# adaLN's first products and column sums in four 32-row places, and attention's scores of a head pair in two 64-row places of TensorE's array

## The chip, the cores and the metric

The kernel runs on one core of one Trainium2 chip. A core has a matrix engine (TensorE, PE in the profile), three engines for element-wise work (VectorE, DVE; ScalarE, ACT; GpSimd, POOL) and queues that start DMA transfers (SP's above all). Each engine works through its own list of instructions in order and waits on semaphores for the others. The metric is the time of one execution on the device in microseconds, the median of several runs.

## What is computed

A trunk of two layers over 512 latent tokens (a grid of 8 rows by 64) and 256 context tokens, width 1024. In each layer a vector per stream (latent or context) is turned into shift, scale and gate of two sub-layers, which is what is called adaLN here:

```python
mod_lat = (silu_c @ ada_w[i] + ada_b[i])[:, None, :]      # ada_w[i]: 1024 x 6144
mod_ctx = (silu_cc @ ada_w[i] + ada_b[i])[None, None, :]
h_lat = modulate(rmsnorm(x, norm_g[i, 0]), sh1, sc1)      # x * (1 + scale) + shift
```

Layer 0 mixes tokens by attention beside a spatial gating unit, layer 1 by retention; each is followed by a gated feed-forward part with a convolution over three tokens. In attention each of eight heads of width 64 takes a softmax over a window of the grid (with a bias and a mask) together with all context keys; context tokens attend to each other:

```python
s_nb = einsum('brqhd,brkhd->bhrqk', qg, k_blk) * scale    # window, + bias, masked
s_cx = einsum('brqhd,bchd->bhrqc', qg, k_ctx) * scale     # context keys
p = softmax(concatenate([s_nb, s_cx]))                    # one softmax over both
```

All data is float32.

## The kernel before, in words

PE multiplies float32 in two ways here. A *native* f32 matmul takes the operands as they are. The other form takes operands rounded to a shorter type (fp32r): a value x is split into hi, its rounded part, and lo = x - hi, by `split` (line 170): ACT writes hi (L171), DVE writes lo (L172). `mm3` (L216 to L218) then sums hi·hi, hi·lo and lo·hi, three matmuls for one product. Tokens are in six tiles of 128 (0 to 3 latent, 4 and 5 context); the contraction dimension lies on the 128 rows of the array.

The stages, in the order of the span: the first products of adaLN with the input projection of the gating unit (`sgu`, to about 150 us), attention (to about 345 us), feed-forward of layer 0, retention, feed-forward of layer 1.

**First products** (`ada_first`, L246). Shift and scale of the first sub-layer are needed before any projection. They are made in four quarters q of the width, each with n = 0 (shift) and n = 1 (scale), each from two weight tiles of 128 x 1024 (kp = 0, 1) holding four blocks k of the contraction. The stationary operand is the conditioning vector's block for both streams, two columns wide (`cs`, L266), the moving one 256 columns of weights; eight matmuls k = 0..7 add up into rows 0 and 1 of a PSUM tile `ad`. Quarters 0 and 1 are native. Quarters 2 and 3 split the weights into `ah` and `al` (1024 wide, on ACT and DVE) and use four columns `c4` (hi and lo of both streams) at L268 and L269. Then ACT copies the rows to `mr` (L273), two small transposes turn them into columns (`adt`, L276), and DVE adds the bias (L284, L286) into `ab`. The products of quarter q + 1 are laid between the projection matmuls `ug` of quarter q in `sgu`; `first_h` scales and splits the tokens for quarter q.

**Later column sums** (`ada_half`, L311). The other shifts, scales and gates are made in the background, a half (512 columns) at a time: DVE multiplies weight tiles by the conditioning vector, one scalar for each row, and adds them up in `acc` (128 x 512, one for each stream, L326). What is left is a sum over the 128 rows. For shifts and scales (12 halves; 8 with two streams, 4 with one) `acc` is split, and matmuls with a two-column selector `sel` (L364) add hi and lo of each stream into row s of `ac`; ACT copies the rows (L366), four transposes (`at`, L370) make columns of them, DVE writes `ab` (L375, L377). Gates are summed with a matrix of ones (L347, L348). These jobs (`bg`) lie between the pieces of `sgu`, attention, both feed-forward parts and retention.

**Attention** (L909). Heads come in pairs j that share a projection: q, k, v of a pair are 128 rows, 64 for each head. `take_qk` (L997) splits them from PSUM, 64 rows at a time: for each head a tile q with hi in rows 0 to 63 and lo in rows 64 to 127, a tile `ka` with k's hi in both halves, and `kb` with k's lo in both, the second half copied by POOL (L1021). So one matmul with `ka` and one with `kb`, each over all 128 rows, give all four products of hi and lo (`score`, L1066, L1067). A block b of a head is 128 query positions: blocks 0 to 3 take 256 window keys and 256 context keys, block 4 the context's own scores, each two matmul pairs into one bank of PSUM (tag B, two banks). DVE adds bias and mask (L1103), finds the least (L1113), ACT takes the exponential (L1122). `weigh` (L1126) follows two blocks later: four transposes (L1136, L1160), a copy by ACT (L1137, L1162), and the product with v in native f32, 64 columns wide, blocks 0 and 1 into rows 0 to 63 of the PSUM tile `o` and blocks 2 and 3 into rows 64 to 127 (L1144 to L1151), once per head; `oc` (L1167) for block 4. The result is split into `at`, 64 rows at a time.

**rms** (L405) adds two partial sums of squares on POOL (L408); POOL then takes the power (L389).

**Order.** The program text gives an order of instructions; `queue` (near the end) replaces each engine's order, and that of the DMAs it starts, by the one in the packed table `ORDER`: for each of PE, DVE, ACT, POOL and SP a list of steps through its instructions.

Of the kernel before, what the change touches and what calls it, by code (L numbers as in the profile page):

```python
# [18 lines left out]
P = 128  # L19
# [37 lines left out]
oBE^h?c}z-ak`$vB|Q9&PqQv3mYD&$*Wq*>fawyZ``woEv$%$z$0HPo&TJgIy{;Zb3sPgTFSB(y41P{#JEHS5aELB=Z}vnav-s}pg0oO(mKLA80q
|Y!J6!ILpC|FO5O*R$9ecKaYBR5RCZvzDi$4G#W`eqf=vRf8Q33#al-=|V4l#%!%0tN|XP9#&R&@D=;l=Jns9HoYdkWwtJb8QLm6O@vc9AJ(*d!0
+_I^7usKHWk>G0od_dhszlPwu%59|Nf@9-s(S@aX>O0oSu+kS%^Bb58|CcO?{WW9cceQ5~MQDdHr-hVU^-=zpPN1gVavHjuLPJ9`=3mf9uxAf_ZS
YSDsAHa4Tt|9@)&~!HO%IdM$Vg7-G&kp>}Pe%DZ2mi_?qg5m4u_~z-e33KZZ#npD4!)OmVVAx1RJ8cv`LH|7O!u|-JRcn#Mb)Fn;vwcL^RZ(?iS0  # L60
+T(zOV7!W@zhd)M|jxR350iLo`)2k0;xS%Pu6nrUvV1j8LYHIJ&SL^3^*&;)(#5ZR-+!d=+f&I8m--%L$vXTmJ*hT||XrVZMkaPW7@P|v_;2X^|k
{?A|Ih6gwoeLpZ^_?g6#(uVBet}k<MaJv)wA5B;Z{Cq-VATmBtijaCSodQk>H*8wB(kq`FiWLVMj8LtypHF9DV$h12aIijz#Wlu~97wc0A78N%Ay
cC5Z2Wz4oYr2Cr20lywx8qP|1YuZ{yr<h!^4+e0cOZ{Y+6zRc+j_=6a9JTA?x^dN~3bqDGp*Cz<0Rsa&&O+tGHV#{^?*g-{w|NXRghvt(*BB1t-Y
%Je8fvUvQB}=Q>=^=;q!1qfd|3MgGQFgN~P2h`ZXE6P3t$661kM?!1zjecY-!C-W0%v#zvawJ>t?{Cnb98`G!t!8q~vdAv|vg55M`WR^jm%_=|n@
xc+92E!h{njJqY_ow>%Spl7nY_s3$>6P0P986E$a&gE@6PS&^;t5Pe8*5lrXoE*CcSn?WJ*Gc-hLy={4&+F-h1xm?_hs$>J$ZZ4IvGJ^CA6De$v|
2|G^id6a4K`?*dVT~rBV0!0W-cZLM+9Rdv8QtkHSNK#@af=CQLxsSsm+;ebAlBT4Mo@9^R}(1b@JxUrx4bactPhs`>DhN%5u{OFp8tTiX{Oixa|W
M%#LD{6u`uhd<9H`5qqJVo1M`hO1a_>F!xJ`Ga}kB|usl{LY%v-gfMpAA(n53NQW)-sxAlMBeE@sYIIb3@-J<2peo+ae(8y{iK0~zMT;i8ujU&fu
_d7*CVmwx2wsxD<i2`qdpGxo*jp(N0O{8vhnxcJt0pT3A9Bf-}9sCNNly8388;{qr-{aI$k8u?CdYxo2EH#YNfStxZ6n~)J$Q$bs8du0^3`5R-}<
Oi>2YD^44P`K_MRh=Gk1z@xW**bSq0TGHN-4aP%qe!Hj%beI~TCIF!1pG&Q6Rrkm9vF>XYxsmokGVhs;;V?%#GytF|_;Oz3=1c^U4;2gI}R8LLlv
!CQQvCV~q3%ijnk0mBq>4(35W<Q;?)VFBj1S{Q*>Hc);mSal<Lny~i)3{6(nH0VGxVhhXkjbaM&;4a=3wxLG>yNpZYyW^_>C=<XuoExl`agZ=RfG  # L70
d$6!nKWZu?0x_Hd?saPrM=41T_E?9n^ZmXkvQb0~G+cS*(1B_Fwh#1IU=_(Ggtj%!``=^D+kma{Q!g#l<%0al)eBcC3K`-8(M+L=FhG5YbFaVM4}
{{en}Z$w2g2hA)isZ_<_`bu0Q8m%FuH00SkTG>a)N69{*`p&9r`)S1lp5yjv;w=4kK4sx|u1Xpe9^`$fGJ&Ap5D!}ze<gAW#yw7aA)V*rkd`+yEv
}b*gd605%1^i-bMTD2UuYSf`T8r&6?@q@)X5cnCyD1y6`S?)sQv*rQw;eUdE!p>d%=ii;6&OylVc4(3r!w97L&w8OoQ8P)shV04GvG;GwE(u2}<>
KF4Ea843$xNVn0j$Bd(vD-+=HomX@vDEW=wCOnyY*hh#Y6UV)!&D`ps0K8Z!xyXRD5g7>{$@T#Vn2B>>!z4Ssf`aP#$Br_gq@5j#zgN(yMc#LAj(
{XSqkV?PoJW3&wlKFrLPgKdnnKI37qV)P$x>Wh8pA9{e55<^^#I@A{>R-P708b+hy~Yh=>wWN3f@^Awjy?YT%{bEsCa_1c6a1a%_Rq!|{jCY4<VX
GEf5pL<xW%Xn3#`<dOlP*Ami`$x-f4co-3iXc-w*BY68rz)Qy+v^3UA$O*i3ekz?jKQSXdd99WWrAwo)c|=IqJa@X`;%M9y$q_O=)C2|e9C&hnqV
w^~SC`DCTuTmk7V+K=OY|HS13(6t;<j^ge6e!@MUsm1N9O^AeFkMH(nu3sfM2>+k$0*wuDDK@c}B6H7|5cUVL_ndm0_*wOiZF`bqJqvG(ihfp6E-
`cIw&`4c6?=p7b|#l`DsaFU;N!-DJBWNqYc+>XGGezmTpa989%v{uu_$<NU!rs4>WFFE%=zsPxxPYKq?r`)o{FB-jSt6}YEGXiXQ6Es@+IIAB0H$
QUws%Ce_#o$*SI0oJ)A?yZ*j@<Nr30Cvd2K*<<gs0``&bYNIv-^S>yXSUcK=#{Q3l!E5+@^N$XA~4gW?K-1Po)HuK)B<2?a`$L?bwJ`u@G?s@)KI
QEQsj+LwSAdcYye1=PLyp_{yCyl;?h%QGjP|!SX+<bg_nAG87zs-#}Mla7f^Vnm>b>4Sndv1<NM$BQn%2M9q$CA7L4VTM0?j8ladvb*HFpOuxQ|Y  # L80
3vWh+@9<GwXM{B%oM_hVll80=q4$wqUe$cS1v38!o)|Bxsep*(P@d52^SYHHwP)9J`hM1=ZuzpA)5NPN%atueOJ|H>@m>tx7)5&^2(uvL$?42Hzv
`I+SjmFY>1dB=zM0o&J;sUePhlpB=C;6KxytE2QFX7MYvwB+&J;M8x#N4^<V(vT{?6tkL@R1CA31>~Hok*E5R<iFm(=`VBeCda<z^ZCRl70bz3u_
WQ(?@nvL&B$oZoQ-J_!<onNmf28pdCST8=&+cwY0U#e$ai)`jPWwh4LKAm=Kg!OTC|dY?H3q<9v8t7R=kngUi5y*_qY|jzj8v1MYYQ;ovAwZ>dUW
lNvieo1QW?(%F4SY1l-|Aq7TC5VS7yBYh@pmn@k)Ha*?C|#z0b-Kb{}GGc=hkwoJ@X{w?nP&(Y?0xsfaOV0gAG`G++(;^$o~${x>xNwR=PpNv5|G
s1~sv6Q}&z3*$>ZEG|yPoQ{}zQirKG1U(!{WdU;`K*ovoJpoAmwiTY<18}<hSq(kyca%{1?{U@idl=%aA$&nygYJb^vV44SW1AHo=v3|Cl$$W*Sg
# [12 lines left out]
@RhJV~xSMsS6MB#F2{nOH<Pc^FVI9uU*?TtyIqtxiv9DV@z~i*GmTwMVbR1^v?fm!@r8;;pA560L%uF!$7P2=)>Vj<&gh-fUukIJ(NOwH)Ym+IRV
#E3l3(93EVC4Y;PlV-hRSy$EpOy6N4hvcUv_M{^eh9Ve!s?;kyeW3ojTOlX<xQPT+w0#m=l9o`PBDiI~sF<yF1C{)VEMIaAQN4*8lz56M0^C?2fG
f$)C8+!Cd7i@KL{X)cP9bZ>#NA5CpLpQ{3c=*97uiPkHdB9~N1nb5n_&NS@!k@WUCI~%516&zJnMdzhup#g=iSSRnXv<eFi<%mkg2^7GAPC_cBTX  # L100
S@;lxS&dPaQrekol|Qcc;zweS{3POl&e6&sCD1xavuiD)Kh(YqaLp#!9f{-CvMU2`2)c5S~_^a{nprnLa`3v_)(t{@avOWi3`23gQ-T(s+%jV3b+
r&vQAq+vnBkOU;G8!VuyyyHreE=pEi1If{49n=cmOY{l``rCrxbtOaMWxTK&Al%dn0@`<1kt?>_5YQE5rR)`~a;4mIbg_<?x}MT&)I(FYH0t<)sY
|{=Od=xI5)#ZQ$O&9p^xR6twE+Wx?!qBuMnfeBw%PInvEYjmA`B*mLeD5VEmQYv^<`zr@_d_CnhnI*Dq5p260d3zjEp8Cv!{~gyj0{#WhJCuo7T`
mExf&NNq9TAb8wc)7G#;0iY1*`rnev%lFXZ7yJ9;owW#AdB0_IirVYN=F|DFT`4TOb$Vv@kzhu<G;2reo08CXW3KR`Qqh$%>k1Sod&k``GgiXiB6
`)xhU6zb8-=6o%%nZ;>1iolRK~F{uF$G>glEZ8QBV1ySG%h_D1<)*2*BD+g!%-OoAs-TSG%eq3AqOG{)+M52AUX~2U@(bhgW=1R4(y7Q`3)5!AmI
hsb=-=q2N=);-wvrLI|x0lMHs=NJdd|P5kzc8WT=JnvkHn-^`{gar|Q^>jbT`(RMUzjcd?7{n5XCN1*y6;->HU3o`h=P8*OvhI&!K^N=HtKz`%f+
b!7(VYL`-BKFZ|oe@ByV2r^WspxyJJ5eOje9MUUvE(mvaZKN_PaxU}&Rh)%3L0X3ft*D0<dei#uN}JAILJU@_)Q7Mp*vi7qH@R}C%Qae{wK-BMDy
TkR<SQ7^ghnq0b0%2Ai=x5gj;lmyW|b9mIV2V6q5UoqprZl=o)N%UBr$*o?2nvy*+A}Cu#kQr{);XRL6D<cnAAgo%VNMIo2aV|K@}}ryQzkCrBb#
8pGb=22L;p*MoLMqF9Pw}4b$ck+=3#4xT;`uL~m8pMqLmcP-VnC3_PNsdZOxxrOgnCqf55p*n~HU#i$PUcBqM=n^F?GL{-*Wih{IRP@&QmXdt7tF
bBak8KS`#QQL;i^OCP2N@_Z<`2y3lCF;B&;b?kL6%gFeFcpL>ks4@zNO~3If{stkl1UWw9-^rsAx@K*3R+<64z87mqGyVL%n*a5R^WNBY{+ONk_k  # L110
# [28 lines left out]
class Trunk:  # L139
# [106 lines left out]
    def ada_first(self, q, pool, native, tag):  # L246

        S, V, T = self.S, self.V, self.T
        ab = self.ab[0, 0]
        c = slice(2 * q, 2 * q + 2)  # L250
        m = 2 if native else 4
        for n in range(2):
# [22 lines left out]
            for i in range(2):  # L275
                T.transpose(pt[:, i, :], mr[:m, i * P : (i + 1) * P], self.ident[:m, :m])  # L276
# [1769 lines left out]
```

## Time and profile before

| | |
|---|---|
| median of 3 runs | 1785.72 us (1785.25 to 1786.01) |
| the profiled execution | 1785.76 us, span 1784.0 us |
| mean granted TensorE clock | 0.997 |
| first products `ad` | 11.4 to 62.9 us |
| scores `s` | 173.8 to 327.3 us |
| column sums `ac` | 144.2 to 1336.1 us |
| HBM read, written | 191.80 MB, 39.85 MB |

The profile is one execution, taken by the hardware profiler. "Busy" of PE holds for matmuls that overlap: a row's duration runs from its start to its modelled end, and the next begins long before it. In the timeline each row has the start, the duration, the engine, the line, the operation, out<-in by the program's names, the stationary operand as rows*columns, the moving one as rows x columns. PEld is the loading of stationary operands.

### The profile page before, as it was taken

What the parts mean: (1) busy time and instruction counts of PE and PEld (TensorE: products, weight loads), DVE (VectorE), ACT (ScalarE), POOL (GpSimd) and SP (SyncE); (2) the same over time, 40 slices, a digit from 0 to 9 for tenths busy, and PEclk for the clock granted to TensorE, in tenths of its full rate; (3) what the DMA queues carried; (4) which work ended last, traced back from release to release, by engine and by line L of the source; (5) the groups of instructions that cost most, each with busy time, mean ns of one, the idle gap of its engine ahead of it and who ended that gap; (6) DMA issues with size and microseconds to landing.
All of it is one profiled execution on the core that took longest, in us unless ns stands there. A gap on an engine that the chain in (4) does not pass through costs nothing.

```text
span 1784.0 us, 28774 instructions
## 1 busy us (share of the span) xinstructions
PE 1748.3 (98%) x11024; PEld 1578.7 (88%) x11024; DVE 1388.2 (78%) x2363; ACT 1017.5 (57%) x1882; POOL 340.1 (19%) x462
## 2 busy tenths in 40 slices
PE   7999999999999999999999999999999999999997
PEld 4898888799998999999899998998999789999996
DVE  3887886898887787889867666666655799998887
ACT  6633567776555555655665434433444577766773
POOL 1101322230132322222221001101001200222221
PEclk9999999999999999999999999999999999999999
DMA  8345331364687877886734332332322235887764
GB/s 304 116 133 165 99 110 45 106 180 118 171 174 174 173 174 155 164 178 161 257 126 125 118 113 71 119 95 81 97 71 60 107 122 147 214 216 185 180 145 130
DMA packets 84398, 253.44 MB, mean 142 GB/s; under 512 B 11026, under 2 KB 11538, under 8 KB 84260
## 3 DMA queue, kind: packets, MB, share of 16 engines
q1 hardware_dynamic: 55044, 191.27, 33.7%
q0 software_dynamic: 26912, 51.95, 17.1%
q10 hardware_dynamic: 2304, 8.39, 1.2%
q8 instruction: 86, 1.41, 0.3%
q14 instruction: 52, 0.43, 0.1%
HBM read 191.80 MB, written 39.85 MB: 130 GB/s over the span
## 4 chain that ended last, share of the span: by engine, by line
PE 89%; DVE 5%; ACT 3%; DMA 1%; issue 1%; POOL 1%; SPq 0%; DVEq 0%; POOLq 0%; ACTq 0%
PE px L215 11%; PE wf L216 4%; PE wf L217 4%; PE wf L218 4%; PE rn L217 4%; PE rn L216 4%; PE rn L218 4%; PE py L215 4%; PE px L216 2%; PE px L217 2%; PE px L218 2%; PE py L218 1%; PE py L217 1%; PE py L216 1%; PE ug L216 1%; PE ug L217 1%
## 5 line engine op out<-in xcount | busy, mean ns | idle before, releaser
L326 DVE SCALAR_TENSOR_TENSOR acc<-ar,cs,acc 128x512 f32<-128x512 f32 x256 | 190.5, 758 | 11.1 <-DMA ar<-in_adaw 4.3
L216 PE MATMUL rn<-rwv,h0c 128*128 128x256 f32 x384 | 107.8, 281 | 0.0
L217 PE MATMUL rn<-rwv,h0c 128*128 128x256 f32 x384 | 107.5, 281 | 0.0
L218 PE MATMUL rn<-rwv,h1c 128*128 128x256 f32 x384 | 107.2, 280 | 0.0
L1734 POOL DMA_DIRECT2D yf<-yp x64 | 56.0, 963 | 265.1 <-ACT yp L1730 237.7
L1574 ACT ACTIVATE pre<-px 128x256 f32<-128x256 f32 (+2 forms) x160 | 56.0, 369 | 78.0 <-PE px L215 55.9
L1587 DVE SCALAR_TENSOR_TENSOR cv<-pre,cw,cv 128x769 f32<-128x769 f32 (+1 forms) x88 | 77.3, 882 | 27.5 <-ACT cv L1586 26.9
L1586 ACT ACTIVATE cv<-pre,cw 128x770 f32<-128x770 f32 (+1 forms) x88 | 80.9, 925 | 21.5 <-DVE g L172 11.4
L1730 ACT COPY yp<-wf 128x512 f32<-128x512 f32 x118 | 68.4, 584 | 41.8 <-PE wf L218 34.2
L215 PE MATMUL px<-blk,wb 128*128 128x384 f32 (+1 forms) x480 | 79.2, 309 | 1.1 <-ACT pre L1574 1.1
L215 PE MATMUL px<-hs,wc 128*128 128x384 f32 (+1 forms) x480 | 78.9, 309 | 1.0 <-ACT pre L1574 0.8
L1590 DVE SCALAR_TENSOR_TENSOR cv<-pre,cw,cv 128x769 f32<-128x769 f32 (+1 forms) x88 | 76.8, 881 | 0.9
L215 PEld LDWEIGHTS px<-hs,wc 128*128 128x128 f32 x480 | 73.5, 188 | 4.1 <-ACT pre L1574 1.6
L215 PEld LDWEIGHTS px<-blk,wb 128*128 128x128 f32 x480 | 72.8, 188 | 3.8 <-ACT pre L1574 1.6
L171 ACT ACTIVATE wc<-q 128x512 fp32r<-128x512 f32 x80 | 49.8, 629 | 44.1 <-PE py L215 20.7
L216 PEld LDWEIGHTS rn<-rwv,h0c 128*128 128x128 f32 x384 | 72.4, 189 | 1.2 <-issue 0.2
L218 PEld LDWEIGHTS rn<-rwv,h1c 128*128 128x128 f32 x384 | 72.5, 189 | 0.7
L217 PEld LDWEIGHTS rn<-rwv,h0c 128*128 128x128 f32 x384 | 72.4, 188 | 0.9
L1734 POOL DMA_DIRECT2D yd<-ypg x48 | 48.4, 1053 | 122.1 <-ACT ypg L1730 104.6
L218 PE MATMUL rn<-rwg,h1c 128*128 128x256 f32 x256 | 71.3, 279 | 0.0
L217 PE MATMUL rn<-rwg,h0c 128*128 128x256 f32 x256 | 71.1, 279 | 0.0
L216 PE MATMUL rn<-rwg,h0c 128*128 128x256 f32 x256 | 71.1, 279 | 0.0
(1545 smaller groups left out, 6328.4 us busy)
## 6 DMA issues: line engine op xcount, KB each, us to landing
ar<-in_adaw SPq DMA_DIRECT2D x96, 512.0 KB
yf<-yp POOLq DMA_DIRECT2D x64, 256.0 KB, 4.3
yd<-yp POOLq DMA_DIRECT2D x54, 256.0 KB, 5.5
yd<-ypg POOLq DMA_DIRECT2D x54, 256.0 KB, 5.5
fin<-xd SPq DMA_DIRECT2D x8, 512.0 KB
xn<-in_x SPq DMA_DIRECT2D x6, 512.0 KB
xb<-in_x SPq DMA_DIRECT2D x6, 512.0 KB
xd<-xb ACTq DMA_DIRECT2D x6, 512.0 KB
```

What stands on the lines that cost most here:

```text
L171: self.S.activation(hi, src, AF.Copy)
L215: mm = lambda *p, **k: self.T.matmul(*p, skip_group_check=True, **k)
L216: mm(out, lhs[0], rhs[0], start=first, stop=False)
L217: mm(out, lhs[0], rhs[1], start=False, stop=False)
L218: mm(out, lhs[1], rhs[0], start=False, stop=last)
L326: V.scalar_tensor_tensor(out=acc[s], in0=raw[:, kk * 512 : kk * 512 + 512], scalar=self.cs[:, 8 * s + k : 8 * s + k + 1], in1=acc[s], op0= ...
L1574: S.activation(pre[:, i, c : c + w], ps[:, b : b + w], AF.Copy, scale=scale)
L1586: S.activation(d, s, AF.Identity, scale=w1, bias=b)
L1587: V.scalar_tensor_tensor(out=d[:, 1:W], in0=s[:, 0 : W - 1], scalar=w0, in1=d[:, 1:W], op0=ALU.mult, op1=ALU.add)
L1590: V.scalar_tensor_tensor(out=d[:, 0 : W - 1], in0=s[:, 1:W], scalar=w2, in1=d[:, 0 : W - 1], op0=ALU.mult, op1=ALU.add)
L1730: S.copy(v, ps)
L1734: G.dma_start((yd[t] if first else y[t])[:, o], v, accum_op=ALU.add)
```

## The change

1. `ada_first` is native for all quarters. The stationary operand `c32` has 32 columns (two of them the streams, the rest zero), and the four blocks k of a weight tile go to the four groups of 32 rows of PSUM, g = 0..3, each summing over kp only. The four partial rows are added by a product with `pick` (128 x 2), which also turns rows into columns. The splits, L268/L269 and `mt` go; raw weight buffers are six instead of four.
2. `ada_half` takes native sums of `acc` with a 32-column `one` into the four groups (stream and part of the columns), without splits, then one or two full transposes.
3. `take_qk` splits 128 rows at once into hi and lo tiles; `scores` takes three products of 64 rows (hi·hi, hi·lo, lo·hi) for each head, the two heads in rows 0 to 63 and 64 to 127 of the array in turn, into two banks. Tiles go head by head within a block; `weigh` multiplies with v for both heads at once, after blocks 1 and 3 and for block 4, and its splits are 128 rows.
4. `rms` adds on DVE.
5. `ORDER` is new.

The diff, cut to its core:

```diff
+        self.one = self.cp.tile([P, RB], F32, name="one", tag="one")
+        G.memset(self.one, 0.0)
+        G.memset(self.one[:, 0:1], 1.0)
+        self.pick = self.cp.tile([P, 2], F32, name="pick", tag="pick")
+        V.tensor_reduce(out=self.pick, in_=self.ident.rearrange("p (g z) -> p z g", z=RB)[:, 0:2, :], axis=AX.X, op=ALU.add)
...
-                raw = pool.tile([P, 1024], F32, name=f"ar{n}{q}{kp}", tag="raw", bufs=4)
+                raw = pool.tile([P, 1024], F32, name=f"ar{n}{q}{kp}", tag="raw", bufs=6)
...
-                    if native:
-                        T.matmul(ps[:2, :256], self.cs[:, k : 16 : 8], raw[:, o], start=(k == 0), stop=(k == 7))
-                    else:
-                        T.matmul(ps[:4, :256], self.c4[:, k, :], hi[:, o], start=(k == 0), stop=False)
-                        T.matmul(ps[:4, :256], self.c4[:, k, :], lo[:, o], start=False, stop=(k == 7))
+                for g in range(4):
+                    T.matmul(
+                        ps[RB * g : RB * g + RB, :256],
+                        self.c32[:, 4 * kp + g, :],
+                        raw[:, g * 256 : g * 256 + 256],
+                        start=(kp == 0),
+                        stop=(kp == 1),
+                    )
...
-                T.transpose(pt[:, i, :], mr[:m, i * P : (i + 1) * P], self.ident[:m, :m])
+                T.matmul(pt[:, i, :], mr[:, i * P : (i + 1) * P], self.pick, start=True, stop=True)
...
-            T.matmul(ps[:2], self.sel[:, i // 2, :], sp[i // 2][i % 2], start=(i == 0), stop=(i == n - 1))
+        cn = 4 // streams
+        w = 512 // cn
+        for g in range(4):
+            s, c = g % streams, g // streams
+            T.matmul(ps[RB * g : RB * g + RB, :w], self.one, acc[s][:, c * w : c * w + w], start=True, stop=True)
...
-        for i in range(4):
-            T.transpose(pt[:, i, :], row[:2, i * P : (i + 1) * P], self.ident[:2, :2])
+        for j in range(jn):
+            T.transpose(pa[:, j, :], row[:, j * P : (j + 1) * P], self.ident)
...
-        self.G.tensor_scalar(out=w, in0=ss[:, 0:1], scalar1=ss[:, 1:2], scalar2=EPS, op0=ALU.add, op1=ALU.add)
+        self.V.tensor_scalar(out=w, in0=ss[:, 0:1], scalar1=ss[:, 1:2], scalar2=EPS, op0=ALU.add, op1=ALU.add)
...
+                self.c32 = fp.tile([P, KD, RB], F32, name="c32", tag="c32")
+                G.memset(self.c32, 0.0)
+                S.activation(self.c32[:, :, 0:2], self.cs.rearrange("p (s k) -> p k s", s=2), AF.Copy)
...
-            tiles = [(h, b) for h in range(8) for b in (0, 1, 2, 3, 4)]
+            tiles = [(2 * j + s, b) for j in range(4) for b in (0, 1, 2, 3, 4) for s in range(2)]
...
+                    if step % 2 == 0:
+                        self.scores(j, step // 2, pr, heads[2 * j : 2 * j + 2])
...
-            G.tensor_copy(kb[H1], kb[H0].bitcast(F32))
+        self.split(*[x[:, 0:512].rearrange("p (a r l) -> p a r l", a=4, r=8) for x in q], src)
+        self.split(*[x[:, 512:] for x in q], pr["x"][:, 0, :])
+        self.split(*[x[:, 512:] for x in k], pr["x"][:, 1, :])
...
+        pss = [self.ps(f"s{2 * j + s}{b}", "B") for s in range(2)]
...
+            for n, (x, y) in enumerate(((qh, kh), (qh, kl), (ql, kh))):
+                for s in range(2):
+                    r = slice(64 * s, 64 * s + 64)
...
+                    T.matmul(o, x[r, cols], m, start=n == 0, stop=n == 2)
...
-            if b < 3:
+            if s == 0 or b % 2 == 0:
                 return
...
+                for s in range(2):
...
+                    T.matmul(po[64 * s : 64 * s + 64, c], vc(i, s), m, start=n == 0, stop=n == 4)
...
+            for s, p in enumerate((self.pc0, pcT)):
+                T.matmul(po[64 * s : 64 * s + 64, :], vc(4 + kt, s), p[:, kt * 256 : kt * 256 + 256], start=(kt == 0), stop=(kt == 1))
```

More of the change, by code (lines that the diff above doesn't have):

```diff
@@ L57 @@
[L57 to L61, printed above, removed]
@@ L244, in ada_unit_src, with ada_first @@
         return self.a["adaw"][r : r + P]
-    def ada_first(self, q, pool, native, tag):
+    def ada_first(self, q, pool, tag):
         S, V, T = self.S, self.V, self.T
```

351 lines of the change are left out of this document (153 added, 198 removed).

## The prediction

> **What bounds the kernel now.** I read the page first, then busy time by stretches, then single tiles and the timeline of TensorE (PE). The page's span and shares:
>
> ```profile
> span 1784.0 us, 28774 instructions
> PE 1748.3 (98%) x11024; PEld 1578.7 (88%) x11024; DVE 1388.2 (78%) x2363; ACT 1017.5 (57%) x1882; POOL 340.1 (19%) x462
> PE 89%; DVE 5%; ACT 3%; DMA 1%; issue 1%; POOL 1%; SPq 0%; DVEq 0%; POOLq 0%; ACTq 0%
> ```
>
> The second row is busy time by engine, the third the chain that ended last. PE is the bound over the whole span, so a microsecond of PE issue time removed is worth nearly a microsecond, and work taken from VectorE (DVE) or ScalarE (ACT) is worth only the PE stalls that it ends. The run profiled took 1785.76 us, 1.76 more than its span; the median of the runs shown is 1785.72, so I set the sum against 1785.8. By stretches (time; then busy of PE, weight load, DVE, ACT, POOL; clock; DMA share; GB/s):
>
> ```profile
> 10.00:15.00 5.00, 4.38 (x16) 2.43 (x17) 1.76 (x3) 3.17 (x10) 2.22 (x6) 1.00 1.03 420
> 30.00:65.00 35.00, 35.00 (x186) 23.79 (x185) 26.93 (x57) 24.64 (x40) 0.00 (x0) 1.00 0.68 230
> 172.00:345.00 173.00, 168.18 (x1133) 139.78 (x1132) 137.30 (x374) 114.77 (x283) 47.58 (x64) 1.00 0.27 85
> ```
>
> The granted clock is 1.00 in all three. The first products of adaLN lie between 11 and 63 us. At 10 to 15 us the loads fill the DMA engines (share 1.03); from 30 on PE never rests and nothing else is full. Attention (172 to 345) leaves PE idle for 4.8 us.
>
> **The change, part by part.** A busy matmul row is longer than its share of PE, because matmuls are pipelined; I price by the distance between starts. These rows count what goes (engine, line, tile: ns least/median/most; first and last start):
>
> ```profile
> L266 PE MATMUL ad<-ar,cs x64: 378/379/634, 11.4 to 36.6; 128*2 128x256 f32 x64
> L268 PE MATMUL ad<-ah,c x32: 276/276/281, 41.6 to 62.8; 128*4 128x256 f32 x32
> L269 PE MATMUL ad<-al,c x32: 274/276/280, 41.7 to 62.9; 128*4 128x256 f32 x32
> ```
>
> ```profile
> L364 PE MATMUL ac<-ah,sel x20: 387/397/478, 144.2 to 1335.9; 128*2 128x512 f32 x20
> L364 PE MATMUL ac<-al,sel x20: 388/397/472, 148.1 to 1336.1; 128*2 128x512 f32 x20
> ```
>
> The program has 32 native f32 matmuls at L266 (two of four quarters q, two halves n, eight k) and the trace 64 records: each f32 matmul counts twice; transposes and the rounded (fp32r) ones count once. Now their distances, and what a change of the array's form costs:
>
> ```profile
> 30.99 0.40 PE L218 MATMUL ug<-ug,h1a 128*128 128x512 f32 x1
> 31.23 0.40 PE L216 MATMUL ug<-ug,h0a 128*128 128x512 f32 x1
> 31.55 0.59 PE L266 MATMUL ad<-ar,cs 128*2 128x256 f32 x2
> 32.08 0.50 PE L217 MATMUL ug<-ug,h0a 128*128 128x512 f32 x1
> 32.41 0.39 PE L218 MATMUL ug<-ug,h1a 128*128 128x512 f32 x1
> ```
>
> ```profile
> 33.41 3.62 PE L266 MATMUL ad<-ar,cs 128*2 128x256 f32 x16
> ```
>
> ```profile
> 41.63 0.28 PE L268 MATMUL ad<-ah,c 128*4 128x256 f32 x1
> 41.75 0.27 PE L269 MATMUL ad<-al,c 128*4 128x256 f32 x1
> ```
>
> ```profile
> 48.28 0.39 PE L218 MATMUL ug<-ug,h1a 128*128 128x512 f32 x1
> 48.60 0.28 PE L276 MATMUL adt<-ident,mr 4*128 4x4 f32 x2
> 48.81 0.50 PE L218 MATMUL ug<-ug,h1a 128*128 128x512 f32 x1
> 49.14 0.40 PE L216 MATMUL ug<-ug,h0a 128*128 128x512 f32 x1
> ```
>
> Sixteen records in 3.62 us, the last lasting 0.38: 0.216 us each. A 512-wide fp32r matmul steps by 0.23, a 256-wide one with four columns by 0.115. Around the two L266 records the steps are 0.32 (0.09 too long), then 32.08 - 31.55 = 0.53 for two records of 0.216 (0.10 too long), then 0.33 (0.10 too long): entering and leaving the narrow form costs **0.28 us**. The two small transposes adt (L276) between 48.28 and 48.81 cost 0.53 - 0.23 + 0.10 = 0.40. That two column places run side by side is in this trace:
>
> ```profile
> 212.68 0.38 PE L1144 MATMUL o<-ptall,vn 128*64 128x256 f32 x1
> 212.69 0.38 PE L1145 MATMUL o<-ptall,vn 128*64 128x256 f32 x1
> 212.90 0.38 PE L1144 MATMUL o<-ptall,vn 128*64 128x256 f32 x1
> ```
>
> Two f32 records in two 64-column places start 0.01 apart and the next pair 0.22 later: two in the time of one. Four 32-column places aren't shown. Bounds: four in the time of one (0.43 per group of four matmuls, two records each) or only two by two (0.86). I take 0.45, because the second place costs 0.01 here.
>
> *First products, q = 1 to 3* (PE full). Old: 32 L266 records x 0.216 = 6.9, two narrow stretches x 0.28 = 0.6, 64 x 0.115 = 7.4, six adt pairs x 0.40 = 2.4; together 17.3. New: 3 quarters x 2 n x 2 kp = 12 groups x (0.45 + 0.28) = 8.8; twelve products with `pick`, two records each, full array so without a change of form, taken at 0.085, a quarter of the set of four small transposes at 170.13 below (0.34 us; bounds 0 and 0.12, the 256-wide step): 24 x 0.085 = 2.0; together 10.8. **-6.5.** If DMA, DVE or ACT took over the bound there, it would be 0; row 30 to 65 shows DVE at 26.9 of 35 before eight 1024-wide splits leave it, and DMA at 0.68, so they don't while the stretch shrinks by a fifth.
>
> *First quarter*, before 30 us: 32 records, 6.9, become 4 x (0.45 + 0.28) = 2.9, which is -4.0 on PE. But the loads still have to land, and six raw buffers in place of four only help later quarters. Bounds 0 and -7 (the start of ug pulled up to where the loads end); I take **-3**. The memset and copy that fill `c32` are one operation each on POOL and ACT, which the first row shows with 2.2 and 3.2 of 5 us busy; they cost nothing if they are through before the first product at 11.4, and else delay it by themselves, within these bounds.
>
> *Later column sums*, twelve halves (eight with two streams, four with one). Old: 40 x 0.23 = 9.2, and twelve sets of four small transposes:
>
> ```profile
> 170.13 0.41 PE L370 MATMUL at<-ident,arow 2*128 2x2 f32 x4
> 170.47 0.50 PE L216 MATMUL pv<-h0a,wv 128*128 128x512 f32 x1
> 170.81 0.39 PE L217 MATMUL pv<-h1a,wv 128*128 128x512 f32 x1
> ...
> 232.14 0.60 PE L1136 MATMUL pt<-ident,sc 128*128 128x128 f32 x4
> ```
>
> One set takes 0.34 to the next start, 0.09 to enter as before and 0.11 after: 0.54, in all 6.5; old sum 15.7. New: eight groups at 0.45, four half as wide at 0.23, twelve changes x 0.28, and 8 x 2 + 4 = 20 full transposes at (0.60 - 0.27) / 3 = 0.11: 4.5 + 3.4 + 2.2 = 10.1. **-5.6.** They lie in attention, both feed-forward stages and retention, beside a full PE. The twenty splits that also go were on ACT and DVE, off the path: 0.
>
> *Scores.* Rows and distance:
>
> ```profile
> L1066 PE MATMUL s<-ka,q x80: 275/281/386, 173.8 to 327.1; 128*128 128x256 f32 x80
> L1067 PE MATMUL s<-kb,q x80: 276/281/394, 177.6 to 327.3; 128*128 128x256 f32 x80
> ```
>
> ```profile
> 207.63 0.28 PE L1066 MATMUL s<-ka,q 128*128 128x256 f32 x1
> 207.75 0.28 PE L1067 MATMUL s<-kb,q 128*128 128x256 f32 x1
> ```
>
> Old: 160 x 0.118 = 18.9. New: 20 blocks x 12 = 240 matmuls of 64 rows. No 64-row matmul is in the trace. Bounds: pairs side by side as the column places do, 120 x 0.118 = 14.2, or one after the other, 28.3. I take 14.2, from the pair at 212.68, the only row with two places. The 20 blocks each change the form, while `o` and `oc` need it 12 times in place of 16 (three per pair of heads, not two per head): 16 x 0.28 = 4.5. Net **-0.2**: nothing. o and oc have the same columns to stream.
>
> *Splits of q, k and at* run on 128 partitions instead of 64, so about half the instructions; POOL's copy of kb goes. All is on DVE, ACT and POOL, so it is worth stalls only:
>
> ```profile
> PE s L1067 <- POOL kb L1021: 1.2, 1, 1.2
> ```
>
> Of attention's 4.8 us I take **-2**: this wait, and part of those behind DVE's split of `at`. Bounds 0 and -4.8. An added wait: a block of scores now needs both banks of tag B, so PE stands until the softmax reads of both heads of the block before are done; behind it in PE's queue stand transposes, projections, and through them the next softmax. A block comes each 173 / 20 = 8.6 us, so there is cover; 0 while projections remain, late in the last pair perhaps 1.
>
> *rms* moves from POOL to DVE: one small operation fewer between engines, but DVE now waits for ACT's squares at that place in its order, and behind it stand the residual's and the splits' operations, for which PE's next transposes wait. Bounds -3 and +3, I take **-1**. The new order table moves every queue, SP's loads too; no row prices it, 0.
>
> Sum: -6.5 - 3 - 5.6 - 0.2 - 2 - 1 = -18.3; 1785.8 - 18.3 = **1767.5 us**.
>
> The Trainium skill (TensorE: Matmul & The Clock Gate, "Measured speedup vs the span model") gives 3.07 times for four row places and 2.38 for three column places, not 4 and 3. An estimate from it: 28 groups of four at 0.56 instead of 0.45 would give back some 3 us, and the sum would be 1770.5. The pair at 212.68 shows no such loss for two places.
>
> **The rivals.**
>
> 1. *Row places take turns.* Then scores cost 28.3, +14.1: **1781.6**. For it: all the trace's weight loads for fp32r scores are 128 columns wide, and there are 240 instead of 160. Against it: the column pair at 212.68, and four 128-column loads of `at` that begin within the 0.34 us of that set, under 0.09 each. The Trainium skill (same page, "LDWEIGHTS") says that a load's time goes by its columns, whatever its rows, 107 ns for 128; by that 240 loads in a row would take 25.6 us, near this rival; the set at 170.13 is faster than that.
> 2. *Slower: each turn between the two row places is a change of form.* Two places alternate in every pair of matmuls, so 240 x (0.118 + 0.09) = 50 us in place of 14.2: +35.7, **1803**. It decides from (14.2 + 18.3) / 240 = 0.135 us per 64-row matmul; above that the change is slower. For it: the 0.09 seen at 31.55. Against: the alternating places at 212.68 pay nothing.
> 3. *The first stage is held by loads.* Then -6.5 and -3 shrink to nothing: **1777**. For it: the DMA share of 1.03 at 10 to 15 us. Against: 0.68 later.
> 4. *Four column places pack only two by two*: the twenty full groups of q = 1 to 3 and of the sums at +0.43, four at +0.22, together 9.5 (the first quarter's are mostly hidden): **1777**. The change then doesn't do what it says.
> 5. *More than counted*: loads and a shorter q-k split let the first quarter give 7 and attention all its 4.8, and blocks standing next to `o` share changes of form: **1758**.
>
> **How the numbers follow.** About 0.2% (3.6 us) can be told from no change. Chances: the forecast (1762 to 1774) 0.45; rival 3 0.12; rival 4 0.08; rival 1 0.10; rival 2 0.10; rival 5 0.15. Rival 1 ends at the edge of "same", so half of it counts there. Faster 0.45 + 0.12 + 0.08 + 0.05 + 0.15 less 0.02 for orders that lose: 0.83; same 0.06; slower 0.11. The range 1755 to 1782 leaves out rival 2 and the tails.
>
> **What would show it.** Right: `ad` records in fours, start within 0.03 us, next four 0.22 later; score records in pairs 0.01 apart and 0.12 to the next pair; the last `ug` before `gg` 8 to 14 us earlier; no wait on `kb`. Wrong: score records 0.12 or 0.2 apart (rivals 1, 2), `ad` waiting for DMA (3), `ad` in pairs (4), or PE waiting for softmax before `s`, which I priced at nothing.

## The result, and the profile after

The changed kernel took **1788.35 us** (median of 20 runs, 1785.98 to 1789.93), the kernel before 1786.05 on the same chips (20 runs, 1785.06 to 1788.34): 1.0012 times the time of before, 95% interval 1.0005 to 1.0019. So 18 us less were forecast, and it is 2 us slower, within 0.2%. First the page of the changed kernel, span and busy time by engine:

```profile
span 1787.0 us, 28706 instructions
PE 1743.1 (98%) x11116; PEld 1572.2 (88%) x11116; DVE 1356.0 (76%) x2328; ACT 976.4 (55%) x1786; POOL 311.5 (17%) x412
```

PE is busy for 5.2 us less, and yet the span is 3.0 longer: idle PE (span less busy) went from 35.7 to 43.9. The stretches that the prediction looked at, in the changed kernel:

```profile
10.00:15.00 5.00, 3.29 (x14) 2.57 (x14) 1.63 (x3) 3.20 (x9) 0.29 (x2) 1.00 1.03 420
30.00:65.00 35.00, 35.00 (x220) 26.09 (x220) 19.71 (x46) 20.84 (x35) 0.04 (x1) 1.00 0.56 186
172.00:345.00 173.00, 172.75 (x1175) 135.66 (x1174) 120.95 (x338) 92.37 (x224) 32.97 (x49) 1.00 0.27 85
```

Attention's idle 4.8 us are gone (173.00 less 172.75). Where the time went is read from milestones: the start of a tile's first or last matmul in each trace. "All edits" is the kernel of the experiments below in which only the order is altered.

| start, us | before | after | all edits |
|---|---|---|---|
| first `ug` | 30.2 | 29.2 | 27.5 |
| last `ug` | 115.2 | 108.8 | 107.0 |
| last score `s` | 327.3 | 322.0 | 315.6 |
| last `watd`, attention's output product | 366.3 | 357.8 | 351.6 |
| first quarter of all `px`, feed-forward 0 | 560.5 | 560.6 | 550.5 |
| last `wf0C`, its output | 896.6 | 892.7 | 882.3 |
| last `rn`, retention | 1397.1 | 1395.9 | 1385.5 |
| last `wf1C`, feed-forward 1 | 1774.1 | 1777.5 | 1760.9 |

At 358 us the changed kernel leads by 8.5 us. The lead is gone by the first quarter of `px`, is back at 3.9 at the end of feed-forward 0 and is lost again. (In feed-forward, `px`, `py` and `pz` are PSUM tiles of the input products, `hs`, `hb` and `blk` the split tokens, `wa` to `wd` the split weights, `fo` those of the output product `wf`.) So the question is what happens at the starts of the two feed-forward stages. The waits of PE from 385 to 420 us:

```profile
PE py L219 <- DVE wb L173: 4.7, 1, 4.7
```

and ScalarE's timeline just before:

```profile
390.28 0.85 ACT L1571 ACTIVATE cv<-cv 128x770 f32<-128x770 f32 x1
397.13 0.85 ACT L172 ACTIVATE hs<-sb 128x768 fp32r<-128x768 f32 x1 [6.00 <-DMA sb<-sa]
...
398.67 0.64 ACT L172 ACTIVATE wc<-q 128x512 fp32r<-128x512 f32 x1
399.20 0.64 ACT L172 ACTIVATE wb<-s 128x512 fp32r<-128x512 f32 x1
399.72 0.85 ACT L172 ACTIVATE g<-cv 128x770 fp32r<-128x770 f32 x1
```

ScalarE works in order. At 391 us it comes to `hs`, whose data a transfer brings only at 397.1, and stands for 6.00 us. Behind `hs` stand `wc`, `wb` and `g`, whose inputs have long been there. VectorE comes to its part of the tiles late in its turn:

```profile
402.08 0.95 DVE L173 TENSOR_TENSOR hs<-sb,hs 128x768 fp32r<-128x768 f32 x1
403.88 0.68 DVE L173 TENSOR_TENSOR wb<-s,wb 128x512 fp32r<-128x512 f32 x1
```

The second row is the low half of the `wb` that PE needs; its high half was ready since 388.2 (ScalarE, 387.62). But it stands behind the low halves of `wc` and `hs`, and so behind ScalarE's wait. PE, which reached `py` at 399.55, starts again at 404.62. In the kernel before, ScalarE has these four in the same order and also stands ahead of `hs`, but VectorE has the low half of that `wb` ahead of `wc` (rows of both engines, in order of time):

```profile
398.00 0.69 DVE L172 TENSOR_TENSOR wb<-s,wb 128x512 fp32r<-128x512 f32 x1
399.97 0.85 ACT L171 ACTIVATE hs<-sb 128x768 fp32r<-128x768 f32 x1 [2.69 <-issue]
401.25 0.62 ACT L171 ACTIVATE wb<-s 128x512 fp32r<-128x512 f32 x1
401.37 0.69 DVE L172 TENSOR_TENSOR wc<-q,wc 128x512 fp32r<-128x512 f32 x1 [1.82 <-ACT wc L171]
```

There PE comes to `py` at 405.62 and doesn't wait for it. So what is new at this place is VectorE's order and a PE that comes 6 us earlier; on ScalarE `hs` stood ahead of these three already. The same place in the changed kernel by stretches (PE, weight load, DVE, ACT, POOL; then the granted clock):

```profile
396.13:399.55 3.42, 3.42 (x21) 3.42 (x20) 0.20 (x1) 2.42 (x6) 0.00 (x0) 1.00 0.11 18
399.55:402.96 3.41, 0.34 (x2) 0.01 (x1) 3.41 (x6) 3.11 (x5) 0.00 (x0) 1.00 0.00 0
402.96:406.37 3.41, 1.75 (x5) 1.66 (x6) 3.11 (x5) 3.41 (x5) 0.00 (x0) 0.50 0.02 5
406.37:409.79 3.42, 3.42 (x13) 3.42 (x12) 3.42 (x5) 3.06 (x8) 0.00 (x0) 0.50 0.85 256
409.79:413.20 3.41, 3.41 (x21) 3.38 (x20) 2.99 (x4) 1.39 (x3) 0.00 (x0) 1.00 0.13 53
```

The pause is paid a second time: for 6.83 us after it PE has half its clock, 13 matmuls in a stretch that holds 21 at full clock. At 1455 us, the start of feed-forward 1, the pattern is the same: ScalarE is idle for 4.00 us ahead of an `hs`, and here it is the new table that puts `hs` ahead of the reads `pre` of products that were finished by 1448.8 (the kernel before reads two of the three, `pf110b` and `pf100b`, at 1445.47 and 1449.65, ahead of its `hs` at 1451.60):

```profile
PE py L216 <- ACT pre L1552: 3.5, 1, 3.5
```

and half clock from 1457.68 to 1464.51. Before the change there is one such stretch ahead of the end (1424.44), after it there are three.

### The profile page after: what moved, and what is told of

It is laid out like the page before. It is cut to its first block, busy times and chain, and to the rows that moved or that the text cites. A ratio compares the mean times of both kernels' runs of the same rounds, so it can differ in the third digit from the quotient of the medians.

```text
span 1787.0 us, 28706 instructions
## 1 busy us (share of the span) xinstructions
PE 1743.1 (98%) x11116; PEld 1572.2 (88%) x11116; DVE 1356.0 (76%) x2328; ACT 976.4 (55%) x1786; POOL 311.5 (17%) x412
## 5 line engine op out<-in xcount | busy, mean ns | idle before, releaser
L1565 DVE SCALAR_TENSOR_TENSOR cv<-pre,cw,cv 128x769 f32<-128x769 f32 (+1 forms) x88 | 77.4, 883 | 29.4 <-ACT cv L1564 29.2
L1564 ACT ACTIVATE cv<-pre,cw 128x770 f32<-128x770 f32 (+1 forms) x88 | 80.6, 923 | 15.7 <-DVE g L173 8.0
L173 DVE TENSOR_TENSOR wc<-q,wc 128x512 fp32r<-128x512 f32 x80 | 54.7, 686 | 17.5 <-ACT wc L172 17.4
```

The source lines that it names most:

```text
L173: self.V.tensor_tensor(out=lo, in0=src, in1=hi.bitcast(F32), op=ALU.subtract)
L1564: S.activation(d, s, AF.Identity, scale=w1, bias=b)
L1565: V.scalar_tensor_tensor(out=d[:, 1:W], in0=s[:, 0 : W - 1], scalar=w0, in1=d[:, 1:W], op0=ALU.mult, op1=ALU.add)
```

## The experiments

**Theory.** The parts of the change do what they say. The new table `ORDER`, which the prediction priced at 0, gives their gain back: it has `hs` ahead of work that is ready, and it splits blocks of scores. **Rivals.** The starts of the feed-forward stages are held by transfers whatever the order; the row and column places don't run side by side; rms on VectorE holds the stages' ends.

All order edits use one hook in `queue`: an instruction x (by its number in its engine's program order) is put right behind another.

```diff
+            for x, behind in MOVES.get(e, ()):
+                row.remove(x)
+                row.insert(row.index(behind) + 1 if behind is not None else 0, x)
```

### 1. `hs` later at the start of feed-forward 0

```diff
+    "Activation": [(376, 363), (375, 376), (387, 374)],
+    "DVE": [(549, 545)],
```

(363 is `g`, 374 and 375 `hs`, 376 `cv`, 387 `fo00h`; on VectorE 549 is the low half of `wb`.)

> The changed kernel with four entries of its order table moved, all at the start of the first feed-forward stage (about 390 us): on ScalarE the split hs<-sb that waits 6.00 us for a transfer goes behind wc, wb and g, and fo00h goes up by one; on VectorE the low half of wb goes from behind the first hs to ahead of wc. Theory (the new order table gives the gain back here): TensorE's wait of 4.7 us at 399.55 goes, and with it the stretch of 6.8 us at half clock, 3.4 us; 8 us off 1788.3, so about 1780, 1779 to 1784 if hs itself becomes the next late thing. Rival (the transfer sets the pace whatever the order): the wait moves to the first use of hs, the time stays within 1 us of 1788. Rival (the gain of the first 390 us is lost later whatever happens here, to something that runs at its own pace): 1788 as well, but with the wait gone.

1783.53 us, 0.9983 of before (0.9973 to 0.9992): 0.0029 below the changed kernel's 1.0012, which is **5.2 us**. PE's waits from 385 to 420, and two of the same stretches:

```profile
PE pz L217 <- ACT wa L172: 1.0, 1, 1.0
PE wf L217 <- ACT fo00h L172: 0.8, 1, 0.8
```

```profile
399.55:402.96 3.41, 2.60 (x14) 1.92 (x12) 1.96 (x4) 2.98 (x5) 0.00 (x0) 1.00 0.03 7
402.96:406.37 3.41, 2.24 (x12) 1.88 (x12) 3.41 (x5) 3.36 (x9) 0.00 (x0) 1.00 0.70 213
```

The wait and the half clock are gone (1.00 in both rows). The rivals, under which the time stays at 1788, are out. 5.2 came instead of 8: two waits of 1.0 and 0.8 took the place of the one, and probably the slow stretch of the changed kernel had hidden part of what was late next. The run moves entries of both engines, so it doesn't tell what ScalarE's and VectorE's moves are worth alone.

### 2. The same at the start of feed-forward 1

```diff
+    "Activation": [..., (1273, 1249), (1269, 1248), (1268, 1269), (1267, 1268), (1272, 1256)],
```

> The kernel before this one, with five entries moved at the start of the second feed-forward stage as well (about 1450 us): on ScalarE the three hs<-sb splits go behind the reads of pf110b, pf101b and pf100b and both passes of cv, and the read of py goes ahead of Silu. Theory: the wait of TensorE of 3.5 us at 1455 and the second added stretch at half clock (6.8 us at 1457.7, 3.4 us) go: 5 to 7 us below the kernel with the first edit alone, about 1774. Rival (VectorE's additions of sb, which run up to 1450, set the pace): no more than 1 us below it.

1779.08 us, 0.9961 (0.9946 to 0.9976): **3.9 us** below run 1. From 1435 to 1465 us the longest waits of PE are now:

```profile
PE wf L217 <- ACT g L172: 0.6, 1, 0.6
PE py L216 <- ACT pre L1552: 0.5, 1, 0.5
```

Of the three half-clock stretches only the one near 1420, which the kernel before has too, is left. The two places cost 9 us together.

### 3. The scores without alternation

```diff
+                    row[run] = sorted(row[run], key=lambda x: (x - b) % 2)
```

for each stretch `run` of neighbouring score matmuls of block b: the even head's first.

> The changed kernel with only the order of attention's 240 score matmuls altered: within each stretch of neighbouring score matmuls, those of the even head come first, then those of the odd head, so that almost no two neighbours lie in different 64-row places (146 sets in a row become 209). Theory (neighbours in different row places run at once, about 0.12 us for the two): 63 sets more at 0.107, 6.7 us longer where TensorE is the bound in attention, so the first pz up to 7 us later; of that the 5.07 us wait at 399.55 can hide some, since TensorE then waits less for hs: 1788 to 1795. Rival (the row places take turns, each matmul its 0.107 whatever its neighbour): the span of attention's scores stays as it is, last score matmul within 1 us of 322.0, and the time at 1788.

1791.90 us, 1.0030 (1.0017 to 1.0042), **3.2 us** above the changed kernel; the last `s` starts at 325.7, 3.7 later. One block of twelve in the changed kernel:

```profile
192.10 0.39 PE L1052 MATMUL s<-kh,qh 64*128 64x256 f32 x2
192.32 0.29 PE L1052 MATMUL s<-kl,qh 64*128 64x256 f32 x2
...
192.79 0.29 PE L1052 MATMUL s<-kh,ql 64*128 64x256 f32 x2
193.01 0.50 PE L218 MATMUL pv<-h1a,wv 128*128 128x512 f32 x1
```

and the same block in this run:

```profile
192.44 0.39 PE L1052 MATMUL s<-kh,qh 64*128 64x256 f32 x1
192.66 0.27 PE L1052 MATMUL s<-kl,qh 64*128 64x256 f32 x1
192.78 0.28 PE L1052 MATMUL s<-kh,ql 64*128 64x256 f32 x1
192.79 0.39 PE L1052 MATMUL s<-kh,qh 64*128 64x256 f32 x2
...
193.47 0.27 PE L1052 MATMUL s<-kh,ql 64*128 64x256 f32 x1
193.67 0.50 PE L218 MATMUL pv<-h1a,wv 128*128 128x512 f32 x1
```

0.91 us for the block alternated, 1.23 without. So the row places do run at once, and that is worth time. But the loss is half of what the theory said: in the second fence pairs appear (x2) although six matmuls of one head stand ahead of the other's six. The odd head's first matmul starts at 192.79, 0.35 us after the block's first and ahead of the even head's last three (its weight load, at 192.78, is the second one that waits for a bank). So here PE starts the other place's matmuls ahead of earlier ones.

### 4. The scores of a block together

On top of run 2, the twelve matmuls of each block at the place of the last of them.

```diff
+                end = row[max(row.index(x) for x in block)]
+                i = row.index(end)
+                row[i : i + 1] = [-x for x in block]
+                row = [abs(x) for x in row if x not in block]
```

> The kernel with both stages mended, and in attention the twelve score matmuls of a block put together at the place of the last of them in TensorE's order (in the table 11 of the 20 blocks are split up among other matmuls). Theory (each change between the 64-row form and the full form costs TensorE about 0.14 us, and 17 round trips fewer): 2 to 4 us below the kernel with both stages mended, about 1771. Rival (the table split them up because the softmax or a bank would be late): 0 to 4 us above it.

1774.05 us, 0.9935 (0.9920 to 0.9950): **4.6 us** below run 2. What was paid in the changed kernel is seen at one split block there:

```profile
217.54 0.39 PE L1052 MATMUL s<-kh,qh 64*128 64x256 f32 x2
...
218.00 0.28 PE L1052 MATMUL s<-kh,qh 64*128 64x256 f32 x1
218.20 0.50 PE L217 MATMUL pk<-h0a,wk 128*128 128x512 f32 x1
218.54 0.40 PE L218 MATMUL pk<-h1a,wk 128*128 128x512 f32 x1
218.86 0.38 PE L1052 MATMUL s<-kh,qh 64*128 64x256 f32 x1
218.87 0.49 PE L1052 MATMUL s<-kl,qh 64*128 64x256 f32 x2
```

The one at 218.00 takes 0.20 until `pk`, the first `pk` 0.34, the second 0.32, where 0.12 and 0.23 are usual: about 0.3 for leaving and coming back, and the matmul at 218.00 runs without a partner. The table has 37 such stretches for 20 blocks (12 of them are split up, not 11). The table of before splits blocks too, into 46 stretches for its 40 (one head each); but there the scores are 128x128 like their neighbours, and nothing changes form. Summed over the trace (from the start of the matmul ahead of a stretch to the start of the one behind it, less that first one's usual step) the scores take 27.0 us in the changed kernel and 21.2 in this run. How much of that is form and how much partners that meet again, the run doesn't separate.

### 5. More moves, and the head of the table

```diff
+    "Activation": [..., (364, 357)],
+    "DVE": [..., (536, 542), (1105, 1107)],
```

> The kernel with both stages mended and the scores grouped (1774.05, ratio 0.9935), with three more entries moved. At about 383 us ScalarE's blk<-sb goes ahead of wb and VectorE's low half of the same tile goes up three places, so that the last accumulating transfer starts some 3 us earlier (it was issued at 388.44 and hs began at 392.67). At about 868 us VectorE's fin (line 444) goes ahead of three operations of the next tile. Theory (these places too are set by the order alone): TensorE's waits of 0.9 (wf on fo00h), 1.0 (pz on wa) and 1.7 (htc on fin) go: 2 to 3.5 us less, about 1771. Rival (at both places the work of VectorE and ScalarE is full and something else is late next): within 1 us of 1774.

1774.71 us, 0.9941 (0.9926 to 0.9955): nothing gained. The waits for `fo00h` and `wa` stay at 1.1 and 1.0, that for `fin` at 1.5. Here the rival held: something else is late next.

```diff
+    "SP": [(0, 1), (2, 0), (3, 2), (7, 3), (8, 7), (9, 8), (10, 9), (4, 14)],
+    "Activation": [..., (0, None)],
+    "DVE": [..., (2, 1)],
```

> The kernel with both stages mended and the scores grouped (1774.05), with the head of the order table put back to the order of before: SP loads cc, xn05 and ident ahead of xn00 and xn01, and the first ar ahead of these; ScalarE takes cs first (one table load of 1.28 us less); VectorE scales xn04 ahead of the partial sum wx05. In the changed kernel the first transpose starts at 11.55 us, before at 8.05. Theory (the table's order, with rms on VectorE behind ScalarE's squares, holds the first quarter): first transpose at about 8, first ug 1.5 to 3.5 us earlier, and the end as much, about 1771.5. Rival (the loads hold it: DMA share 0.90 in the first 30 us): the first transpose comes earlier, the first ug stays within 0.7 us of 28.9, and the time at 1774.

1773.26 us, 0.9933 (0.9918 to 0.9948), by itself not told apart from run 4. The traces do tell: the first transposes of run 4, then of this one,

```profile
10.99 2.48 PE L1809 MATMUL ht<-ident,xn 128*128 128x128 f32 x10 [10.99 <-DVE xn L416]
```

```profile
7.90 0.48 PE L1809 MATMUL ht<-ident,xn 128*128 128x128 f32 x1 [7.90 <-DVE xn L416]
```

start 3.1 us earlier, the first `ug` 1.3 (28.9 to 27.6), and the last `wf1C` 1.3 (1763.0 to 1761.7). So the table's head cost some 1 us: over the traces, the first `ug` starts at 27.8 to 29.5 without this edit and at 27.4 to 28.3 with it (run 6's first one, where it is 32.7, left out). What holds the rest of the first quarter isn't shown; PE still waits 10.4 us there for `xn`, as before (10.1), and the DMA share is 0.93 in the first 30 us.

> All edits together: the two feed-forward starts, the grouped scores, the three moves of the run before last and the head of the table. Theory: the gains add, since TensorE is the bound between these places: 1774.05 less 2 to 3.5 less 1.5 to 3.5, about 1768.5. Rival (one of them only moves a wait): 1771 to 1774.

Runs 4 and 5 in one: 1772.81 us, 0.9931 (0.9914 to 0.9947), **faster than both kernels**. A second measurement:

> The kernel with all edits once more, on the same chip as the one with the filled pause, for a comparison of the two: 1772.8 again, ratio 0.9931.

1775.41 us, 0.9939 (0.9926 to 0.9951). Both lie within the interval of run 4, so run 5's edits together aren't told apart from nothing; the rival, that one of them only moves a wait, held.

### 6. The column places, and rms, alone

Both on the kernel with all edits.

```diff
-                        ps[RB * g : RB * g + RB, :256],
+                        ps[:RB, :256],
```

with `start` only at the first of the eight blocks, `stop` at the last, and 32 rows of `mr` and `pick`.

> The kernel with all edits (1772.8), in which the four groups of a first product all add up in one place of 32 columns instead of four (the same number of matmuls with the same operands; 32 rows of PSUM are then read instead of 128, and the product with pick runs over 32 rows). Theory (four column places run at once: 16 records took 1.00 us in the changed kernel): 16 records one after the other at 0.216 take about 3.5, so each of the 16 groups costs 1.25 us more, 12 of them (quarters 1 to 3) beside a full TensorE: last ug 15 us later, and the first quarter up to 5 more, 1788 to 1793. Rival (columns pack only two by two): half of it, 1780 to 1783.

1791.89 us, 1.0036 (1.0022 to 1.0049): 0.0105 above, **18.8 us**. Sixteen records of a first product in the changed kernel, then in this run:

```profile
39.16 1.07 PE L260 MATMUL ad<-ar,c 128*32 128x256 f32 x16
40.16 0.50 PE L217 MATMUL ug<-ug,h0a 128*128 128x512 f32 x1
```

```profile
38.21 3.64 PE L260 MATMUL ad<-ar,c 128*32 128x256 f32 x16
41.78 0.73 PE L217 MATMUL ug<-ug,h0a 128*128 128x512 f32 x2
```

1.00 us to the next start against 3.57: four column places are worth a factor of 3.6. The last `ug` comes 19.9 us later (126.9). The Trainium skill (TensorE: Matmul & The Clock Gate, "Measured speedup vs the span model") has 2.38 for three column places; with 3.6 for four, less is lost here.

```diff
-        self.V.tensor_scalar(out=w, in0=ss[:, 0:1], scalar1=ss[:, 1:2], scalar2=EPS, op0=ALU.add, op1=ALU.add)
+        self.G.tensor_scalar(out=w, in0=ss[:, 0:1], scalar1=ss[:, 1:2], scalar2=EPS, op0=ALU.add, op1=ALU.add)
```

> The kernel with all edits (1772.8), with the small addition of rms back on GpSimd, where the kernel before has it, each ahead of the power that reads it; the rest of the order unchanged. It undoes the fourth part of the change. Theory (the part was priced at -1 us and the traces of the changed kernel show it at nothing): within 1.5 us of 1772.8. Rival (VectorE's order now holds the ends of the stages: TensorE's wait for fin at about 870, 1.8 us, wasn't there before): 2 to 4 us faster, about 1769.5. Rival (the hand-over to GpSimd was slower): 1 to 3 us slower.

1776.73 us, 0.9944 (0.9929 to 0.9959): 2.3 us above all edits by their first measurement and 0.9 by the second, with intervals that overlap. PE's wait for `fin` at about 870 is longer with rms on GpSimd:

```profile
PE htc L478 <- DVE fin L444: 3.2, 2, 2.8
```

where all edits have 1.8. So rms on VectorE isn't what holds the stages' ends. Whether it helps isn't shown.

### 7. The pause at the end of retention

```diff
+    "DVE": [..., (1743, 1741), (1764, 1744), (1753, 1757)],
```

> The kernel with all edits (1772.8), with three entries of VectorE's order moved at the end of retention (about 1408 us), so that the scaled row yr (line 444) for which TensorE's transposes wait 2.8 us is ready about 1.3 us earlier. In both kernels a stretch of 6.83 us at half clock follows this wait. Theory (the half clock comes only when TensorE rests for most of about 3.4 us): the wait falls to about 1.4 us and the half clock goes, 3 to 5 us less, about 1768.5. Rival (the waits behind it, for hb, take its place): 1771.5 to 1773, with the half clock still there.

1773.74 us, 0.9930 (0.9914 to 0.9947): nothing gained. The wait fell from 2.8 to 2.0 us, but two for `hb` (1.1 each) followed it, and the half clock stayed:

```profile
1408.64:1412.05 3.41, 1.41 (x13) 1.20 (x12) 2.82 (x8) 3.41 (x12) 1.17 (x2) 1.00 0.89 286
1412.05:1415.46 3.41, 1.42 (x5) 0.72 (x4) 3.41 (x10) 3.00 (x7) 0.56 (x1) 0.50 0.12 49
```

PE was busy for 1.41 of 3.41 us, 0.41, and the next window has half clock. The last run fills the pause instead; its added transposes change no value of the output.

```diff
+            for d in range(20 if (l, toks[0], kk) == (1, 2, 0) else 0):
+                self.T.transpose(pt[:, d % q, 0:P], self.ident, self.ident)
```

> The kernel with all edits (1772.8), with 20 transposes more on TensorE at about 1409 us, of the identity into places that the next transposes overwrite, so that nobody reads them: 2.2 us of work in the pause of 2.8 us in which TensorE waits for yr. Nothing is taken away; TensorE only has more to do. Theory (the granted clock is set in windows of 3.413 us: one in which TensorE is busy for less than about 0.45 is followed by half clock; in all runs so far those at 0.42 and less were, and nearly all from 0.44 up were not): busy in that window goes from 0.21 to about 0.8, the stretch of 6.83 us at half clock goes, about 3 us less, 1769.5. Rival (the half clock has another cause, the end of the stage or what the transposes do): the time stays at 1772.8 or grows by up to 0.5.

1773.22 us, 0.9926 (0.9912 to 0.9939), 2.2 us below the same kernel without them (1775.41, 0.9939), with intervals that overlap. Of the two profiles' difference, 1.8 us are there before the pause begins (last `wrC`, retention's output product, at 1408.4 and 1410.2), so it can't be put down to the pause. The windows of this run:

```profile
1408.13:1411.54 3.41, 2.19 (x17) 1.83 (x16) 3.41 (x8) 3.06 (x10) 0.48 (x2) 1.00 0.72 233
1411.54:1414.96 3.42, 2.69 (x25) 2.49 (x23) 3.42 (x11) 3.39 (x10) 1.25 (x3) 1.00 0.25 101
```

and of the one without:

```profile
1410.86:1414.27 3.41, 1.09 (x10) 0.85 (x8) 3.41 (x10) 3.41 (x12) 1.10 (x2) 1.00 0.89 304
1414.27:1417.68 3.41, 2.12 (x8) 1.77 (x9) 3.41 (x9) 3.13 (x7) 0.56 (x1) 0.50 0.07 25
```

Busy 0.64 in place of 0.32, and no half clock before the end of the program. In the eight other traces from run 4 on, PE is busy for 0.18 to 0.41 of that window, and half clock follows each time. So useless work kept the clock here. From the last `wrC` to the last `wf1C` it saves at most 0.7 us (353.3 against 354.0, and 353.7 in the first trace of all edits), probably since VectorE is busy for 3.41 of 3.41 us here and sets the pace anyway.

## Why the prediction was wrong, step by step

- **The new order table, "no row prices it, 0": the step that failed.** The edits to the order alone, 22 moves and the blocks of scores put together, bring the time from 1.0012 to 0.9931 and 0.9939 of before: 13 to 14.5 us. In parts: `hs` and the low half of `wb` at feed-forward 0 5.2, `hs` ahead of `pre` 3.9, blocks split 4.6, the head some 1 by the traces. The text treated "no price" as "0" and gave it no bound, though the profile before has what was needed for one: a ScalarE in order that stands for 2.69 us ahead of `hs`, with the low half of `wb` ready only 7 us ahead of its `py` (398.69 and 405.62), and a PE that was forecast to come 10 us and more earlier. The table may also have gained something: two waits of PE in feed-forward 0 of the kernel before, 2.9 us together (`wf` on `yp`, between 540 and 640 us), aren't there in the changed kernel. No run tells why.
- **First products, quarters 1 to 3, -6.5, first quarter -3.** PE's time for `ad` and `adt`, summed as above, went from 25.9 to 15.7, -10.2 where -6.5 and -4.0 were worked out. From first to last `ug` it is -5.4. The first quarter gave 1.0, and 2.7 with the head mended, near the -3 taken. The last `ug` comes 6.4 us earlier, 8.2 with all edits, where 8 to 14 was the sign of being right.
- **Later column sums, -5.6.** PE's time for `ac` and `at` went from 15.7 to 10.1 us: -5.6. Right for PE's time; whether it all reaches the end is the open question below.
- **Scores, -0.2.** Pairs 0.12 us apart and forms at 0.3: right. But the text counted one change of form for each of the 20 blocks, the table makes 37 stretches of them, and 146 sets one after the other in place of 120. Without PE's idle in them the scores took 22.0 us before (18.9 in the sum), 27.0 after and 20.8 with whole blocks: +5.0 where -0.2 was forecast, -1.2 with whole blocks. This too is the table.
- **Splits and stalls, -2.** Attention's idle went from 4.8 to 0.25: -4.6, near the far bound. No wait for softmax came with the second bank in the changed kernel, and one of 0.3 us (`sc`) with whole blocks.
- **rms, -1.** At the kernel with all edits it is -2.3 or -0.9 by which measurement one takes, with intervals that overlap: not told apart from 0.
- **Rivals 1, 2 and 4** (row places take turns, each turn is a change of form, columns pack two by two) are out by runs 3 and 6. The slower side came, but by none of the mechanisms listed for it.

What stays open: with the order mended the kernel is 11 to 12 us below before, not 18. The milestones place the rest behind attention. At the last `watd` all edits lead by 14.7 us; up to there the sum has 6.5 + 3 + 0.2 + 2 and some 2 for the four of twelve column sums that lie ahead of it, so about 14. Behind it the sum has some 4.5 more (eight column sums and rms), and the lead shrinks to 13.2 instead. It falls to 10.0 at the first quarter of `px`, where PE waits for `wa`, `fo00h` and `b` (1.1, 1.0 and 0.9; before 0.8 in all), is back at 14.3 at the last `wf0C`, while the kernel before has its waits for `yp` between the two, and falls to 11.6 at the last `rn`, with waits of 0.8, 0.3 and 0.3 us (`rn`, `rs`, `rt`) from 880 to 960 us that aren't there before. Moves at feed-forward 0 and ahead of retention (run 5) gained nothing; what holds these places wasn't found. Nor was it tried what a better order would do for the kernel before, which has waits of its own (2.9 for `yp`, 3.1 for `sa` at the end of retention); so how much of the 11 to 12 us is owed to the five parts and how much to the moves alone isn't shown.

## What to carry to other kernels

A change to an order written by hand is a change by itself: price it by finding, at each stage's start, the instruction that waits for a transfer, and asking what stands behind it on its engine, and whether that still comes in time when the engine it feeds arrives earlier. A gain upstream lasts only if the next stage's first inputs come earlier too, so follow the lead from milestone to milestone instead of looking at the end alone. Work in a narrow form of the array should stand together, since each split costs a change of form (about 0.3 us here) and partners that no longer meet.

## What was not expected of the hardware

- **The clock is granted in windows.** In every trace the half-clock stretches ahead of the program's end last 3.41 or 6.83 us, and in the changed kernel they start at 402.96, 1423.55 and 1457.68, the second and third 299 and 309 times 3.413 us after the first. Of all windows from 20 us on up to the program's end in the traces of both kernels and of the twelve experiments, the 18 at full clock in which PE was busy for 0.42 or less were all followed by half clock; of the 72 from 0.44 to 0.75 three were (0.49, 0.58 and 0.59). The Trainium skill (TensorE: Matmul & The Clock Gate, "What's actually happening") says that the window is free-running, 3413 ns long, and that one idle window halves the clock. The length agrees; the window needn't be idle, 0.41 busy was enough in run 7.
- **A matmul can start ahead of earlier ones if it is for the other row place** (run 3, at 192.79: the odd head's first, three matmuls ahead of its turn).
